# Two of the turns of a hybrid attention and convolution trunk, taken from TensorE to VectorE and a crossing through memory

## The chip, the cores and the metric

One core of a Trainium2 chip runs the whole program. The metric is device time in microseconds (us) from the first to the last instruction's end, median of several runs; lower is better. The engines are called as in the profile: PE is TensorE (PEld its weight loads), DVE is VectorE, ACT is ScalarE, POOL is GpSimd, and SP issues most of the transfers.

## The reference

A trunk of two layers on 256 tokens of 2048 features, float32. Cut to what matters here:

```
for layer in range(2):
    h = rms_norm(x, norm_g)                                  # 256 x 2048
    q, k, v, g_att, glu_a, glu_b, g_conv = split(h @ w_in)   # seven times 2048 columns
    att    = dilated_mixture(rope(rms(q)), rope(rms(k)), v)  # 16 heads of 128
    att_y  = rms_norm(att, att_out_g) * silu(g_att)          # the gated attention
    u      = glu_a * sigmoid(glu_b)                          # the gated unit
    y      = depthwise_conv(u, 31 taps, causal) + dw_bias
    y      = silu(layer_norm(y, ln_g, ln_b))
    conv_y = rms_norm(y @ w_pw, conv_out_g) * silu(g_conv)
    x      = x + concat(att_y, conv_y) @ w_out
```

## The kernel before

**Products.** Every projection is done in float32 precision by three products of float32r parts: the weights are split into `whi` (ACT, L238) and the rest `wlo` (DVE, L239), the activations into `st_hi` and `st_lo`, 128 features by 256 tokens each, and `whi*sthi + wlo*sthi + whi*stlo` is accumulated. A *tile* is 256 rows by 512 columns of a weight; it takes 12 matmuls of 512 columns (L669). A *group* is 8 tiles: 512 columns of one projection for all tokens. A layer has 40 groups: glu_b, glu_a, v, q, k for each of four column blocks j; then g_conv 0, g_att 0 to 3, g_conv 1 to 3; then o_att 0 to 3, pw 0 to 3, o_conv 0 to 3. There are 640 tiles in all. Weights are loaded by SP into four buffers `raw` (512 KB each); `split(i)` stands three tiles ahead of the products of tile i, and the load that reuses its buffer stands right behind it.

**Turns.** A projection leaves PE with tokens on the partitions. The convolution and the next product need features on the partitions. So the gated unit (`Dt[0]`, written by `ev_glu_a`), q, k, the gated attention (`A[j]`, written by `ev_g_att`), the result of pw and the new x are turned by PE: `transposes` (L280) makes 8 transposes of 128 x 128 for a block of 256 x 512, from where ACT (and DVE for `st_lo`) evict them. The function `to_stationary` does the turn and both parts; it waits until the stationary chunk is vacant, which for the gated attention is during g_conv 3.

**Convolution and norm.** `conv` runs 31 taps for each of four feature tiles of a block on DVE, the first tap as `V.tensor_scalar` (L403), the others as `scalar_tensor_tensor` (L406). Then POOL adds up the means (`ysum`), `ln_square` squares on ACT, `add_squares` sums the squares over features on POOL (L355, L357, into `ssum`), `token_sums` finishes on PE (L366), POOL makes the reciprocal root (`rsqrt`, and `rbc` at L441), PE spreads it (L445), and `ln_silu` makes the stationary parts that pw reads.

**Order.** The instruction streams are written in the order in which the Python code emits them. Between the tiles' products a planner, `Filler`, places everything else: each piece states its cost on an engine in a `Need` (P, V, A, G in us), and is emitted when the planner's clock for its inputs is past and the engine is not more than a horizon ahead (V 4.5 us, A 3.5 us). Each engine runs its stream in order.

Of the kernel before, what the change touches and what calls it, by code (L numbers as in the profile page):

```python
# [30 lines left out]

KS = 2
NSTEP = KT // KS
R_RAW, R_SPLIT = 4, 4
AHEAD = 3

WARM = 10
# [13 lines left out]
class Filler:  # L51
# [7 lines left out]

    def __init__(self, banks, horizon, patience):  # L60
        self.tasks = []
        self.t = dict(P=0.0, V=0.0, A=0.0, G=0.0)
        self.horizon, self.patience = horizon, patience
        self.banks = [(b, 0.0) for b in banks]
        self.count = 0
# [42 lines left out]
    def _fits(self, task):  # L108
        prio, _, _, need, ready = task
        now = self.t["P"]  # L110
        if not need.holds():
            return False
        if need.banks and sum(at <= now for _, at in self.banks) < need.banks:
            return False
        late = 0 if prio < self.patience else 2
        for n, (e, cost) in enumerate(need.time):
            if n == 0 and ready > (now if e == "P" else max(now, self.t[e]) + 0.2):
                return False
            e = "V" if e == "G" else e
            if e in self.horizon and max(self.t[e], ready) + cost > now + self.horizon[e] - late:  # L120
                return False
        return True
# [23 lines left out]
def trunk(ctx: ExitStack, tc: tile.TileContext, x, w_in, q_norm_g, k_norm_g, w_pw, w_out, x_t, gains, params,  # L146
# [8 lines left out]
    def t(shape, name, dt=F32):  # L155
        return sb.tile(shape, dt, name=name)
# [13 lines left out]
    qT, kT = (C[i].rearrange("p (h s) -> p h s", h=4) for i in (1, 2))  # L170
    Dt = [t([128, 2, CH], f"d{i}") for i in range(3)]
    t2 = t([128, CH], "t2")
    sm = [t([128, 384], f"sm{i}") for i in range(4)]
    junk = t([128, CH], "junk", BF16)
    ident = t([128, 128], "ident")
# [19 lines left out]

    acc = [pp.tile([128, CH], F32, name=f"acc{i}") for i in range(4)]
    fill = Filler([pp.tile([128, CH], F32, name=f"ax{i}") for i in range(4)], dict(V=4.5, A=3.5), 5)

    xs = [dr.tile([SEQ, CH], F32, name=f"xs{c}") for c in range(NCH)]

# [65 lines left out]
    def has(*what):  # L266
        return lambda: what in flags
# [6 lines left out]
    def transposes(src, banks):  # L274

        for b in range(2):
            for i in range(2):
                for tt in range(2):
                    e = (2 * b + i) * 128
                    T.transpose(banks[b][:, i * SEQ + tt * 128:i * SEQ + tt * 128 + 128],  # L280
                                src[:, tt, e:e + 128], ident)

    def to_stationary(src, s, c, gain):

        yield Need(2, lambda: vacant[s][c], P=0.9)
        banks = [fill.bank(), fill.bank()]
        transposes(src, banks)
        yield Need(A=1.5, V=1.6)
        p = [b[:, i * SEQ:(i + 1) * SEQ] for b in banks for i in range(2)]
        for i in range(4):  # L290
            S.activation(st_hi[s][c][:, i], p[i], AF.Copy, scale=gain(i))  # L291
        for i in range(4):
            V.scalar_tensor_tensor(st_lo[s][c][:, i], p[i], gain(i), st_hi[s][c][:, i].bitcast(F32),  # L293
                                   op0=ALU.mult, op1=ALU.subtract)
        fill.free(*banks)
        filled(s, c)

    def filled(s, c):
        vacant[s][c] = False
        ready[s][c] = True  # L300
# [17 lines left out]

    def x_chunk(l, c):

        yield from to_stationary(A[c], 0, c, lambda i: ng[:, l * KT + 4 * c + i:l * KT + 4 * c + i + 1])
        fill.add(x_square(l, c), 3, fill.now[4])

    def x_square(l, c):
# [24 lines left out]

    def add_squares(sq, j, *name):  # L350
        for h in range(2):
            yield Need(0, has(*name, j - 1) if j else None, G=1.3)
            half_sq = sq[:, h * CH:(h + 1) * CH]
            if j == 0 and h == 0:
                G.tensor_copy(ssum, half_sq)  # L355
            else:
                G.tensor_add(ssum, ssum, half_sq)  # L357
        flag(*name, j)

    def token_sums():  # L360
# [17 lines left out]
    def ev_glu_a(l, j, ps):  # L378
        yield Need(0, has("ev", l, "glu_b", j), V=1.4)
        for tt in range(2):  # L380
            V.scalar_tensor_tensor(Dt[0][:, tt], ps[tt], rx[:, tt:tt + 1], Dt[0][:, tt],
                                   op0=ALU.mult, op1=ALU.mult)
        flag("ev", l, "glu_a", j)
        yield Need(2, has("conv", l, j - 2) if j >= 2 else None, P=0.9)
        banks = [fill.bank(), fill.bank()]
        transposes(Dt[0], banks)
        yield Need(A=1.0)
        for b in range(2):
            S.activation(uT[j % 2][:, 2 * b:2 * b + 2, PAD:], banks[b].rearrange("p (c s) -> p c s", c=2), AF.Copy)
        fill.free(*banks)  # L390
        flag("glu", l, j)
        fill.add(conv(l, j), 5 + j, fill.now[4])

    def conv(l, j):
        u = uT[j % 2]
        y = Y[j].rearrange("p (c s) -> p c s", c=4)
        w = prm[:, 4 * j:4 * j + 4]
        for k in range(CW):
            for c in range(4):
                if c % 2 == 0:  # L400
                    yield Need(V=0.8)
                if k == 0:
                    V.tensor_scalar(y[:, c], u[:, c, 0:SEQ], w[:, c, l * CW:l * CW + 1], w[:, c, P_BIAS + l:P_BIAS + l + 1],  # L403
                                    op0=ALU.mult, op1=ALU.add)
                else:
                    V.scalar_tensor_tensor(y[:, c], u[:, c, k:k + SEQ], w[:, c, l * CW + k:l * CW + k + 1], y[:, c],  # L406
                                           op0=ALU.mult, op1=ALU.add)
        flag("conv", l, j)
        for c in range(4):
            yield Need(0, has("ysum", l, j - 1) if j else None, G=0.7)  # L410
            if j == 0 and c == 0:
                G.tensor_copy(ysum, y[:, c])
            else:
                G.tensor_add(ysum, ysum, y[:, c])  # L414
        flag("ysum", l, j)
        if j == NCH - 1:
            fill.add(layer_norm(l), 4, fill.now[4])
# [151 lines left out]
    def ev_g_att(l, j, ps):  # L569
        yield Need(0, has("attsq", l, j), A=1.2, V=1.2)  # L570
        for tt in range(2):
            S.activation(Dt[0][:, tt], ps[tt], AF.Silu, scale=rx[:, tt:tt + 1])
        V.tensor_mul(A[j], A[j], Dt[0])
        flag("ev", l, "g_att", j)
        yield from to_stationary(A[j], 0, j, lambda i: prm[:, 4 * j + i, P_ATT + l:P_ATT + l + 1])
        src = x[0, :, j * CH:(j + 1) * CH] if l == 0 else xs[j]
        nc.sync.dma_start(A[j], src.rearrange("(t p) e -> p t e", p=128))

# [6 lines left out]
    def ev_pw(l, j, ps):  # L585
# [6 lines left out]
        if j == NCH - 1:  # L592
# [1 line left out]
            V.tensor_reduce(rsc, ssf, axis=mybir.AxisListType.X, op=ALU.add)  # L594
            rsqrt(rc, rsc, 1.0 / D, 2)
            flag("rc", l)
        yield from to_stationary(y, 1, j, lambda i: prm[:, 4 * j + i, P_CONV + l:P_CONV + l + 1])

    def ev_o_conv(l, j, ps):
        yield Need(0, has("rc", l), V=1.4)  # L600
# [19 lines left out]
    load(2)  # L620
    load(3)
    x_load(2)
    make_identity(nc, ident)
    V.memset(half, -0.5)
    for u in uT:
# [10 lines left out]
                G.tensor_mul(rope[nm + part], rope[nm + part], gbc[:, None, :].to_broadcast([128, 2, DH]))  # L636

    split_first()


    users = {"glu_b": ev_glu_b, "glu_a": ev_glu_a, "v": ev_v, "g_conv": ev_g_conv, "g_att": ev_g_att,
# [3 lines left out]
    for i, (g, s) in enumerate(tiles):  # L645
# [4 lines left out]
            fill.until(has("ev", *groups[g - 2][:3]))  # L650
        for a in range(i + AHEAD if i else 1, i + AHEAD + 1):
            split(a)
            if a == 1:
                x_load(3)
            if a in (1, 4, 6):
                first_chunk((1, 4, 6).index(a) + 1)
        ps = [acc[(2 * g + tt) % 4] for tt in range(2)]
# [80 lines left out]
```

## Time and profile before

| | |
|---|---|
| median of 3 runs | 1853.83 us (1853.01 to 1854.2) |
| the profiled execution | 1854.28 us, of which the span from first to last instruction is 1852.5 us |
| PE busy | 1844.7 us, 8494 matmuls |
| DVE busy | 1397.7 us (75%) |
| ACT busy | 987.4 us (53%) |
| POOL busy | 142.3 us (8%) |
| granted TensorE clock | 1.000 of full speed |
| HBM | 188 GB/s over the span |

Busy time of PE is not work at its peak, since matmuls overlap: the recorded time of one is longer than the step from one to the next. So the chain of what ended last is read beside it. One profiled execution stands for the runs: its time is 0.45 us above their median.

### The profile page before, as it was taken

To read this page: it belongs to the slowest core of one execution; us is meant where nothing else is said; L and a number is where in the kernel's file an instruction comes from. 1 tells how busy PE (TensorE), PEld (TensorE's weight loads), DVE (VectorE), ACT (ScalarE), POOL (GpSimd) and SP (SyncE) were. 2 spreads that over 40 slices of the span, in tenths; PEclk is the share of its full clock that TensorE was granted. 3 is DMA by queue.
4 is the path that set the end of the run, shared out by engine and by line. 5 is a ranking of instruction groups with operands and counts; after the bars stand their busy time and mean duration, and the time that the engine had idled before them with its cause. 6 is when DMAs were issued, how large, how long until landed. Compare 5 with 4: busy or idle time off the path is not lost.

```text
span 1852.5 us, 23729 instructions
## 1 busy us (share of the span) xinstructions
PE 1844.7 (100%) x8494; PEld 1534.4 (83%) x8494; DVE 1397.7 (75%) x2162; ACT 987.4 (53%) x1549; POOL 142.3 (8%) x153
## 2 busy tenths in 40 slices
PE   9999999999999999999999999999999999999999
PEld 6888888888888888888888888888888888888887
DVE  6888889788889876555558888797887998755554
ACT  6465564655644465445444655646556445644542
POOL 0210100200010140000000101002001002100000
PEclk9999999999999999999999999999999999999999
DMA  8655656556566676555666556565565666665564
GB/s 276 211 183 162 189 157 197 183 161 192 162 191 194 193 221 210 194 183 196 208 202 193 183 162 191 159 194 181 161 192 160 194 195 190 213 204 195 176 205 146
DMA packets 180599, 349.97 MB, mean 189 GB/s; under 512 B 11216, under 2 KB 11216, under 8 KB 180480
## 3 DMA queue, kind: packets, MB, share of 16 engines
q1 hardware_dynamic: 178512, 345.09, 59.6%
q0 software_dynamic: 960, 1.77, 0.5%
q8 instruction: 66, 1.08, 0.2%
q10 hardware_dynamic: 1008, 1.59, 0.2%
q14 instruction: 53, 0.43, 0.1%
HBM read 344.21 MB, written 4.19 MB: 188 GB/s over the span
## 4 chain that ended last, share of the span: by engine, by line
PE 99%; DMA 0%; DVE 0%; ACT 0%; ACTq 0%; issue 0%
PE acc L669 94%; PE ax L280 2%; PE ax L517 1%; PE ax L534 1%; PE ax L543 0%; PE ax L542 0%; PE ax L541 0%; PE ax L516 0%; DMA y<-in_x_t 0%; PE ax L366 0%; DVE wlo L239 0%; PE ax L445 0%; PE ax L422 0%; DVE stlo L307 0%; DVE a L602 0%; ACT whi L249 0%
## 5 line engine op out<-in xcount | busy, mean ns | idle before, releaser
L239 DVE TENSOR_TENSOR wlo<-raw,whi 128x1024 fp32r<-128x1024 f32 x639 | 792.0, 1248 | 392.2 <-ACT whi L238 386.0
L238 ACT ACTIVATE whi<-raw 128x1024 fp32r<-128x1024 f32 x639 | 674.6, 1063 | 658.1 <-PE acc L669 480.6
L669 PE MATMUL acc<-whi,sthi 128*128 128x512 f32 x2560 | 822.6, 392 | 2.0 <-ACT whi L249 2.0
L669 PE MATMUL acc<-wlo,sthi 128*128 128x512 f32 x2560 | 814.9, 389 | 0.3 <-DVE wlo L239 0.3
L669 PE MATMUL acc<-whi,stlo 128*128 128x512 f32 x2560 | 814.7, 389 | 0.0
L669 PEld LDWEIGHTS acc<-wlo,sthi 128*128 128x128 f32 x2560 | 480.4, 188 | 101.7 <-DVE wlo L250 0.9
L669 PEld LDWEIGHTS acc<-whi,stlo 128*128 128x128 f32 x2560 | 480.6, 188 | 100.4
L669 PEld LDWEIGHTS acc<-whi,sthi 128*128 128x128 f32 x2560 | 475.8, 188 | 98.0 <-ACT whi L249 3.3
L406 DVE SCALAR_TENSOR_TENSOR y<-ut,prm,y 128x256 f32<-128x256 f32 x960 | 410.1, 485 | 0.0
L414 POOL TENSOR_TENSOR ysum<-ysum,y 128x256 f32<-128x256 f32 x30 | 36.6, 1218 | 240.9 <-DVE y L406 131.6
L479 POOL TENSOR_SCALAR qr<-qss 128x8 f32<-128x8 f32 x16 | 3.1, 197 | 663.7 <-ACT junk L476 663.7
L476 ACT ACTIVATE junk<-acc,rx 128x128 bf16<-128x128 f32 x128 | 47.0, 367 | 8.4 <-PE acc L669 4.8
L486 ACT ACTIVATE d<-acc,qr 128x128 f32<-128x128 f32 x128 | 34.7, 383 | 16.9 <-POOL qr L481 16.9
L291 ACT ACTIVATE sthi<-ax,prm 128x256 fp32r<-128x256 f32 x64 | 25.1, 475 | 30.7 <-PE ax L280 30.7
L293 DVE SCALAR_TENSOR_TENSOR stlo<-ax,prm,sthi 128x256 fp32r<-128x256 f32 x64 | 26.5, 475 | 14.4 <-ACT sthi L291 14.4
L507 ACT ACTIVATE c<-ax 128x512 f32<-128x512 f32 x32 | 17.4, 596 | 33.7 <-PE ax L280 33.7
L530 ACT ACTIVATE sm<-sm,smm 128x128 f32<-128x128 f32 x64 | 28.2, 442 | 6.6 <-DVE smm L525 6.6
L357 POOL TENSOR_TENSOR ssum<-ssum,d 128x512 f32<-128x512 f32 x14 | 28.5, 2036 | 6.5 <-ACT d L435 5.6
L480 POOL TENSOR_TENSOR qr<-qr,half 128x8 f32<-128x8 f32 x16 | 26.3, 1643 | 1.3
L280 PEld LDWEIGHTS ax<-ident,d 128*128 128x128 f32 x192 | 22.4, 140 | 3.2
L280 PE MATMUL ax<-ident,d 128*128 128x128 f32 x192 | 24.9, 273 | 0.0
L476 ACT ACTIVATION_READ_ACCUMULATOR junk<-acc,rx 128x1 f32 x128 | 24.7, 193 | 0.0
(112 smaller groups left out, 666.7 us busy)
## 6 DMA issues: line engine op xcount, KB each, us to landing
raw<-in_w_in SPq DMA_DIRECT2D x447, 512.0 KB, 3.8
raw<-in_w_out SPq DMA_DIRECT2D x128, 512.0 KB, 4.7
raw<-in_w_pw SPq DMA_DIRECT2D x64, 512.0 KB, 4.7
a<-in_x SPq DMA_DIRECT2D x4, 512.0 KB, 5.7
xs<-a SPq DMA_DIRECT2D x4, 512.0 KB, 6.7
a<-xs SPq DMA_DIRECT2D x4, 512.0 KB, 5.6
y<-in_x_t SPq DMA_DIRECT2D x3, 512.0 KB, 7.2
out<-a SPq DMA_DIRECT2D x4, 256.0 KB, 4.9
```

What stands on the lines that cost most here:

```text
L238: S.activation(hi, a, AF.Copy)
L239: V.tensor_sub(wlo[i % R_SPLIT], a, hi.bitcast(F32))
L280: T.transpose(banks[b][:, i * SEQ + tt * 128:i * SEQ + tt * 128 + 128], src[:, tt, e:e + 128], ident)
L293: V.scalar_tensor_tensor(st_lo[s][c][:, i], p[i], gain(i), st_hi[s][c][:, i].bitcast(F32), op0=ALU.mult, op1=ALU.subtract)
L357: G.tensor_add(ssum, ssum, half_sq)
L406: V.scalar_tensor_tensor(y[:, c], u[:, c, k:k + SEQ], w[:, c, l * CW + k:l * CW + k + 1], y[:, c], op0=ALU.mult, op1=ALU.add)
L414: G.tensor_add(ysum, ysum, y[:, c])
L476: S.activation(junk[:, :DH], ps[tt][:, h * DH:(h + 1) * DH], AF.Square, scale=rx[:, tt:tt + 1], accum_out=qss[:, tt, h:h + 1])
L480: G.tensor_tensor(qr, qr, half.rearrange("p (t h) -> p t h", t=2), op=ALU.pow)
L486: S.activation(n[:, tt, h * DH:(h + 1) * DH], ps[tt][:, h * DH:(h + 1) * DH], AF.Copy, scale=qr[:, tt, h:h + 1])
L530: S.activation(s[:, cs], s[:, cs], AF.Exp, bias=m[:, tt:tt + 1], scale=-1.0, accum_out=lsum[:, tt:tt + 1])
L669: T.matmul(ps[tt], xl if n == 2 else xh, lo[:, kk] if n == 1 else hi[:, kk], start=(k == 0 and n == 0), stop=(k == KT - 1 and n == 2))
```

## The change

The gated unit and the gated attention are no longer turned on PE. DVE transposes each 32 x 32 square of the block on its own (`V.transpose`, two instructions of 128 x 512, into a new tile `blocks`), a transfer on SP's queue writes `blocks` to a buffer in memory, `crossing`, and four transfers read it back with the squares in their new places. The planner has a new clock Q for such transfers: the write is emitted when the transposes' planned end is past, the reads 9.0 us after the write, and what uses the result 13.0 us after the reads. The turned block lies as `(a c t j)`, so ACT and DVE read it through a view (`turned`).

With it: the first tap of the convolution goes from DVE to ACT; the sums of squares of the layer norm go from POOL to DVE, with the first copy folded into the first addition; `raw` has five buffers instead of four (room comes from a smaller descriptor scratch of POOL's transfers), so load(4) stands ahead of the first split, and x_load(3) behind it.

```diff
-R_RAW, R_SPLIT = 4, 4
+R_RAW, R_SPLIT = 5, 4
...
-            if n == 0 and ready > (now if e == "P" else max(now, self.t[e]) + 0.2):
+            if n == 0 and ready > (now if e in "PQ" else max(now, self.t[e]) + 0.2):
...
+    crossing = [dr.tile([4, 128, SEQ], F32, name=f"crossing{i}") for i in range(2)]
+    turns = [0, False]
...
+    def turn(src, dst):
+        yield Need(0, lambda: not turns[1], V=1.4)
+        turns[1] = True
+        for tt in range(2):
+            V.transpose(blocks.rearrange("p (b c t j) -> p t c b j", b=4, c=4, t=2)[:, tt],
+                        src[:, tt].rearrange("p (c b j) -> p c b j", c=4, b=4))
+        yield Need(Q=9.0)
+        way = crossing[turns[0] % 2]
+        turns[0] += 1
+        nc.sync.dma_start(way.rearrange("b p x -> p b x"), blocks.rearrange("p (b x) -> p b x", b=4))
+        yield Need(Q=13.0)
+        turns[1] = False
+        for a in range(4):
+            nc.sync.dma_start(dst[:, a * SEQ:(a + 1) * SEQ], way[:, 32 * a:32 * a + 32])
+
+    def turned(z):
+        return z.rearrange("p (a c t j) -> p c t a j", a=4, c=4, t=2)
+
+    def to_stationary_turned(src, dst, s, c, gain):
+        yield from turn(src, dst)
+        yield Need(0, lambda: vacant[s][c], A=1.8, V=2.2)
+        z = turned(dst)
+        hi, lo = (o[s][c].rearrange("p c (t a j) -> p c t a j", t=2, a=4) for o in (st_hi, st_lo))
+        for i in range(4):
+            S.activation(hi[:, i], z[:, i], AF.Copy, scale=gain(i))
+        for i in range(4):
+            for tt in range(2):
+                V.scalar_tensor_tensor(lo[:, i, tt], z[:, i, tt], gain(i), hi[:, i, tt].bitcast(F32),
+                                       op0=ALU.mult, op1=ALU.subtract)
+        filled(s, c)
...
     def add_squares(sq, j, *name):
         for h in range(2):
-            yield Need(0, has(*name, j - 1) if j else None, G=1.3)
             half_sq = sq[:, h * CH:(h + 1) * CH]
             if j == 0 and h == 0:
-                G.tensor_copy(ssum, half_sq)
-            else:
-                G.tensor_add(ssum, ssum, half_sq)
+                continue
+            yield Need(0, has(*name, j - 1) if j else None, V=0.7)
+            V.tensor_add(ssum, half_sq, sq[:, :CH] if j == 0 else ssum)
...
-        yield Need(2, has("conv", l, j - 2) if j >= 2 else None, P=0.9)
-        banks = [fill.bank(), fill.bank()]
-        transposes(Dt[0], banks)
-        yield Need(A=1.0)
-        for b in range(2):
-            S.activation(uT[j % 2][:, 2 * b:2 * b + 2, PAD:], banks[b].rearrange("p (c s) -> p c s", c=2), AF.Copy)
-        fill.free(*banks)
+        z = Dt[0].rearrange("p t e -> p (t e)")
+        yield from turn(Dt[0], z)
+        yield Need(0, has("conv", l, j - 2) if j >= 2 else None, A=1.7)
+        for c in range(4):
+            S.activation(uT[j % 2][:, c, PAD:].rearrange("p (t a j) -> p t a j", t=2, a=4), turned(z)[:, c], AF.Copy)
...
                 if k == 0:
-                    V.tensor_scalar(y[:, c], u[:, c, 0:SEQ], w[:, c, l * CW:l * CW + 1], w[:, c, P_BIAS + l:P_BIAS + l + 1],
-                                    op0=ALU.mult, op1=ALU.add)
+                    if c == 0:
+                        yield Need(A=1.9)
+                    S.activation(y[:, c], u[:, c, 0:SEQ], AF.Identity, scale=w[:, c, l * CW:l * CW + 1],
+                                 bias=w[:, c, P_BIAS + l:P_BIAS + l + 1])
...
-        yield from to_stationary(A[j], 0, j, lambda i: prm[:, 4 * j + i, P_ATT + l:P_ATT + l + 1])
+        yield from to_stationary_turned(A[j], A[j].rearrange("p t e -> p (t e)"), 0, j,
+                                        lambda i: prm[:, 4 * j + i, P_ATT + l:P_ATT + l + 1])
+        yield Need(Q=1.0)
...
-    nc = bacc.Bacc("TRN2", target_bir_lowering=False, num_devices=1)
+    nc = bacc.Bacc("TRN2", target_bir_lowering=False, num_devices=1, dynamic_dma_scratch_size=4096)
```

Three places in the order of instructions. The first is PE during g_conv 3 of layer 0, where the gated attention's first chunk is turned: `a0` is the gated attention, `ax` the banks for turns, `acc` the accumulators. Before:

```order
L669 MATMUL acc3_156<-whi1_94,stlo00_73 128x512
L280 MATMUL ax2_159<-ident_116,a0_85 128x128 x4
L280 MATMUL ax3_160<-ident_116,a0_85 128x128 x4
L669 MATMUL acc2_155<-whi2_95,sthi01_66 128x512
L669 MATMUL acc3_156<-whi2_95,sthi01_66 128x512
```

The same place with the change:

```order
L712 MATMUL acc3_158<-whi1_95,stlo00_73 128x512
L712 MATMUL acc2_157<-whi2_96,sthi01_66 128x512
L712 MATMUL acc3_158<-whi2_96,sthi01_66 128x512
L712 MATMUL acc2_157<-wlo2_100,sthi01_66 128x512
L712 MATMUL acc3_158<-wlo2_100,sthi01_66 128x512
```

The eight transposes are gone, and the products of the next tile follow at once. Of the 352 transposes of L280, 224 are left.

The second place is SP's queue in the group behind the first glu_a of layer 0, where there were only loads of weights. Before:

```order
L224 DMA raw3_92<-in_w_in 128x2x512
L224 DMA raw0_89<-in_w_in 128x2x512
L224 DMA raw1_90<-in_w_in 128x2x512
L224 DMA raw2_91<-in_w_in 128x2x512
L224 DMA raw3_92<-in_w_in 128x2x512
```

With the change:

```order
L228 DMA raw0_89<-in_w_in 128x2x512
L299 DMA crossing0_163<-blocks_112 128x4x256
L228 DMA raw1_90<-in_w_in 128x2x512
L228 DMA raw2_91<-in_w_in 128x2x512
L228 DMA raw3_92<-in_w_in 128x2x512
L303 DMA d0_108<-crossing0_163 128x1x256 x4
L228 DMA raw4_93<-in_w_in 128x2x512
```

The write stands between two loads, and its four reads three loads later; each load stands for one tile.

The third place is DVE in the layer norm of layer 0, from the token sums (`rsc`) to the first stationary part that pw reads (`stlo10`); each `wlo` row is one tile's split. Before:

```order
L369 COPY rsc_137<-ax2_159 128x2
L239 TENSOR_TENSOR wlo3_100<-raw3_92,whi3_96 128x1024
L239 TENSOR_TENSOR wlo0_97<-raw0_89,whi0_93 128x1024
L239 TENSOR_TENSOR wlo1_98<-raw1_90,whi1_94 128x1024
L239 TENSOR_TENSOR wlo2_99<-raw2_91,whi2_95 128x1024
L582 SCALAR_TENSOR_TENSOR a0_85<-acc0_153,ra_134,a0_85 128x512
L582 SCALAR_TENSOR_TENSOR a0_85<-acc1_154,ra_134,a0_85 128x512
L455 TENSOR_TENSOR y0_81<-y0_81,nmean_126 128x1024
```

With the change, the last sums and the same stretch:

```order
L397 TENSOR_TENSOR ssum_130<-d2_110,ssum_130 128x512
L243 TENSOR_TENSOR wlo2_100<-raw1_90,whi2_96 128x1024
L243 TENSOR_TENSOR wlo3_101<-raw2_91,whi3_97 128x1024
L409 COPY rsc_139<-ax2_161 128x2
L243 TENSOR_TENSOR wlo0_98<-raw3_92,whi0_94 128x1024
L243 TENSOR_TENSOR wlo1_99<-raw4_93,whi1_95 128x1024
L243 TENSOR_TENSOR wlo2_100<-raw0_89,whi2_96 128x1024
L624 SCALAR_TENSOR_TENSOR a2_87<-acc0_155,ra_136,a2_87 128x512
L624 SCALAR_TENSOR_TENSOR a2_87<-acc1_156,ra_136,a2_87 128x512
L495 TENSOR_TENSOR y0_81<-y0_81,nmean_128 128x1024
```

Here the chain has moved 16 tiles later, from the eviction of o_att 0 to that of o_att 2. On PE the token sums stood after 227 tiles and the spread root after 231; now they stand after 245 and 247. The first `stlo10` stood behind the split of tile 236 and now stands behind that of 252; pw reads it from tile 256.

## Rows read from the trace of the kernel before

**Rows 1.** The page: busy time of the engines, and granted clock in 40 slices.

```profile
PE 1844.7 (100%) x8494; PEld 1534.4 (83%) x8494; DVE 1397.7 (75%) x2162; ACT 987.4 (53%) x1549; POOL 142.3 (8%) x153
...
PEclk9999999999999999999999999999999999999999
```

**Rows 2.** The page: the chain that ended last, by engine.

```profile
PE 99%; DMA 0%; DVE 0%; ACT 0%; ACTq 0%; issue 0%
```

**Rows 3.** The same chain in order of time: start us, length us, what.

```profile
648.05 0.87 PE ax L280 x8
648.93 5.46 PE acc L669 x24
654.38 0.87 PE ax L280 x8
...
682.00 138.74 PE acc L669 x612
```

**Rows 4.** Instructions by line and shape, PE's transposes: busy us, mean ns.

```profile
L280 PE MATMUL ax<-ident,d 128*128 128x128 f32 x192 | 24.9, 273 | 0.0
...
L280 PE MATMUL ax<-ident,a 128*128 128x128 f32 x96 | 12.4, 272 | 0.0
```

**Rows 5.** Who waited for whom: us in total, times, longest us.

```profile
ACT whi L238 <- PE acc L669: 480.6, 328, 2.6
DVE wlo L239 <- ACT whi L238: 386.0, 290, 3.9
...
PEld acc L669 <- DVE wlo L239: 0.7, 1, 0.7
```

**Rows 6.** Instructions by line and shape, DVE, ACT and POOL.

```profile
L239 DVE TENSOR_TENSOR wlo<-raw,whi 128x1024 fp32r<-128x1024 f32 x639 | 792.0, 1248 | 392.2 <-ACT whi L238 386.0 <-PE acc L669 4.1
L238 ACT ACTIVATE whi<-raw 128x1024 fp32r<-128x1024 f32 x639 | 674.6, 1063 | 658.1 <-PE acc L669 480.6 <-DVE y L406 164.1 <-DVE a L602 9.2
...
L357 POOL TENSOR_TENSOR ssum<-ssum,d 128x512 f32<-128x512 f32 x14 | 28.5, 2036 | 6.5 <-ACT d L435 5.6
L293 DVE SCALAR_TENSOR_TENSOR stlo<-ax,prm,sthi 128x256 fp32r<-128x256 f32 x64 | 26.5, 475 | 14.4 <-ACT sthi L291 14.4
...
L403 DVE TENSOR_SCALAR y<-ut,prm 128x256 f32<-128x256 f32 x32 | 14.3, 494 | 0.0
...
L525 DVE CUSTOM_DVE_ANT_0 sm<-ax,mask 128x128 f32<-128x128 f32 x32 | 9.3, 292 | 4.4 <-PE ax L517 4.1
L389 ACT ACTIVATE ut<-ax 128x512 f32<-128x512 f32 x16 | 8.7, 596 | 16.8 <-PE ax L280 16.8
...
L314 ACT ACTIVATE sthi<-y,ng 128x256 fp32r<-128x256 f32 x12 | 5.1, 495 | 0.0
...
L345 DVE TENSOR_TENSOR ssum<-d 128x512 f32<-128x512 f32 x1 | 0.7, 691 | 0.0
```

**Rows 7.** Busy time by stage, g_att to g_conv 2 of layer 0.

```profile
508.00:636.00 128.00, 128.00 (x567) 106.03 (x565) 113.11 (x183) 57.44 (x62) 9.88 (x9) 1.00 0.65 193
```

**Rows 8.** Transfers: SP's queue (packets, MB, share), issues (KB, us to landing).

```profile
q1 hardware_dynamic: 178512, 345.09, 59.6%
...
xs<-a SPq DMA_DIRECT2D x4, 512.0 KB, 6.7
a<-xs SPq DMA_DIRECT2D x4, 512.0 KB, 5.6
```

**Rows 9.** The tile `raw`: landing of its loads.

```profile
DMA to landing us min/median/max: 3.4/4.2/8.1
```

**Rows 10.** Timeline of PE, DVE and POOL in layer 0's norm: start us, length us.

```profile
669.61 0.95 PE L366 MATMUL ax<-ones,ssum 128*128 128x2 f32 x8
...
672.04 0.15 DVE L369 COPY rsc<-ax 128x2 f32<-128x2 f32 x1
...
673.33 0.40 POOL L441 COPY rbc<-rstd 128x256 f32<-128x256 f32 x1
...
681.39 0.61 PE L445 MATMUL ax<-ident,rbc 128*128 128x128 f32 x4
```

More of the change, by code (lines that the diff above doesn't have):

```diff
@@ L61, in __init__ @@
         self.tasks = []
-        self.t = dict(P=0.0, V=0.0, A=0.0, G=0.0)
+        self.t = dict(P=0.0, V=0.0, A=0.0, G=0.0, Q=0.0)
         self.horizon, self.patience = horizon, patience
@@ L172, in trunk @@
     t2 = t([128, CH], "t2")
+    blocks = t([128, 2 * CH], "blocks")
     sm = [t([128, 384], f"sm{i}") for i in range(4)]
@@ L319, in x_chunk @@
     def x_chunk(l, c):
-        yield from to_stationary(A[c], 0, c, lambda i: ng[:, l * KT + 4 * c + i:l * KT + 4 * c + i + 1])
+        gain = lambda i: ng[:, l * KT + 4 * c + i:l * KT + 4 * c + i + 1]
+        yield from to_stationary(A[c], 0, c, gain)
         fill.add(x_square(l, c), 3, fill.now[4])
@@ L399, in conv @@
             for c in range(4):
-                if c % 2 == 0:
-                    yield Need(V=0.8)
                 if k == 0:
-                    V.tensor_scalar(y[:, c], u[:, c, 0:SEQ], w[:, c, l * CW:l * CW + 1], w[:, c, P_BIAS + l:P_BIAS + l + 1],
-                                    op0=ALU.mult, op1=ALU.add)
-                else:
+                    if c == 0:
+                        yield Need(A=1.9)
+                    S.activation(y[:, c], u[:, c, 0:SEQ], AF.Identity, scale=w[:, c, l * CW:l * CW + 1],
+                                 bias=w[:, c, P_BIAS + l:P_BIAS + l + 1])
+                else:
+                    if c % 2 == 0:
+                        yield Need(V=0.8)
                     V.scalar_tensor_tensor(y[:, c], u[:, c, k:k + SEQ], w[:, c, l * CW + k:l * CW + k + 1], y[:, c],
@@ L596, in ev_pw @@
             flag("rc", l)
-        yield from to_stationary(y, 1, j, lambda i: prm[:, 4 * j + i, P_CONV + l:P_CONV + l + 1])
+        gain = lambda i: prm[:, 4 * j + i, P_CONV + l:P_CONV + l + 1]
+        yield from to_stationary(y, 1, j, gain)
     def ev_o_conv(l, j, ps):
@@ L622, in trunk @@
     x_load(2)
+    load(4)
     make_identity(nc, ident)
@@ L638, in trunk @@
     split_first()
+    x_load(3)
     users = {"glu_b": ev_glu_b, "glu_a": ev_glu_a, "v": ev_v, "g_conv": ev_g_conv, "g_att": ev_g_att,
@@ L652, in trunk @@
             split(a)
-            if a == 1:
-                x_load(3)
             if a in (1, 4, 6):
```

## The prediction

> **What bounds the kernel now.** The page first: PE is busy for 1844.7 of 1852.5 us and its granted clock is full, the higher of its two levels, in every slice [rows 1]. Since recorded matmuls overlap, busy time alone proves nothing; the chain that ended last does: 99% of the span is PE waiting for nobody [rows 2]. So time is won by taking work off PE's stream, and lost only where PE is made to wait. What does an instruction cost there? In the chain in order of time the reader is to see a regular step [rows 3]: in a stretch without anything else 612 products take 138.74 us, 0.2267 us each, so a tile of 12 takes 2.72 us. Where a turn stands in between, its 8 transposes are 0.87 us of the chain, and from one turn's start to the next (24 products between) it is 654.38 - 648.05 = 6.33 us, of which 24 products are 5.44: a turn costs PE **0.89 us**, the 0.02 over 0.87 lying in the products behind it.
>
> Then the waits [rows 5]. PE waited for DVE's split once, 0.7 us. ACT on the other hand waited for PE in 328 of 639 splits: it starts when PE gives a buffer free. Such a split is due three tiles later, 8.16 us; ACT's half takes 1.06 and DVE's 1.25 [rows 6], so about 5.8 us are spare on DVE and 7.1 on ACT. That is the reserve which every delay below must use up before PE stops. DVE is the engine with least of it: 113.11 of 128 us busy in the densest stage [rows 7].
>
> **What comes off PE.** 16 turns: four blocks, two uses, two layers, 128 of 352 transposes. 16 x 0.89 = **14.2 us**. Nothing is put on PE in their place, and its other instructions stay in their order but for the norm's, below. One rule would make more of it. The records give each transpose 272 to 273 ns [rows 4]; 128 of them by that are 34.9 us. But records overlap: 8 of them fill 2.18 us and take 0.87 of the chain. I take the chain; the other is a rival.
>
> **What goes on DVE.** 32 square transposes: no row shows one. Nearest is a pass over 128x512 float32, 0.691 us [rows 6]; half of that, or twice it if filling and emptying the squares don't overlap, are the bounds: 22.1 us, from 11 to 44. The sums of squares: 14 passes of 128x512 at 0.691, 9.7 us, in place of POOL's 28.5. The gated attention's low parts: 64 instructions of 128x128 at 0.292 are 18.7, in place of 32 at 0.475, 15.2: 3.5 more. The first taps go: 14.3 less. In all 21 us more (10 to 43), 1397.7 to about 1419, 77% of a span of 1838. That is a mean; the place matters. A turn puts 1.4 us (0.7 to 2.8) behind glu_a's or g_att's eviction, inside 5.8 us of reserve even at the upper bound, and the planner defers taps when DVE's stream is full. So it costs nothing; without the cover a turn would cost up to 1.4 us. What becomes late is the end of the convolution and with it the norm. In the order the norm's first part for pw is 16 tiles later, and stands behind the split of tile 252 where pw needs it at 256. Splits run three to four tiles ahead, so it is done near tile 250: some 5 tiles, 13 us, remain. It still hides, but of the slack of some 20 tiles most is gone.
>
> **What goes on ACT.** First taps: 32 of 128x256 from SBUF at 0.495 [rows 6], 15.8 us. Copies of the gated unit: another 32, 15.8, for 16 from PSUM, 8.7. The gated attention's high parts keep their count. About 23 us on 987, against 7.1 us of reserve; at most 2 us stand in one piece. Nothing.
>
> **What goes on the queue.** SP gets 16 writes and 64 reads; each round trip is 512 KB out and 512 KB in. Price of a packet: 59.6% of 16 engines over 1852.5 us by 178,512 packets [rows 8] is 99 ns for 2 KB. The crossing moves rows of 1 KB, 512 packets each way; a packet lies between 50 (by bytes) and 99 ns (by count). On 16 engines that is 32 packets, 1.6 to 3.2 us. A load of 16 packets is 1.6 us and lands in 4.2 [rows 9], so 2.6 is fixed and a leg lands in 4.2 to 5.8; the same bytes in 2 KB rows took 6.7 out and 5.6 in [rows 8]. I take 6 to 7. The planner leaves 9.0 and 13.0, so neither SP nor ACT should stand at these transfers. The queue's share rises by 16 x 2 x (1.6 to 3.2) us, 3 to 6 points. Loads issued behind the reads are later by the reads' time; with five buffers a load is issued 5 x 2.72 - 2.31 = 11.3 us before its split can begin (8.6 with four) and lands in 4.2, at worst 8.1, so 3 to 7 us are free, and then the split's own reserve. Nothing at the start: PE's first products wait for the first two transfers and splits, whose place doesn't change. POOL loses 29 us that nobody waited for.
>
> **Sum.** 1854.28 of the profiled execution - 14.2 = **1840.1 us**. That execution is 0.45 us above the median of the runs, from which the same subtraction gives 1839.6. A measurement of this kernel tells about 0.2%, 3.7 us, from no change.
>
> **Rivals.**
> (a) *The norm makes PE wait.* PE takes its instructions in order, so the token sums and the spread root stop it if POOL and DVE are late. Before, from the token sums' end (670.56) to `rbc`'s (673.73) went 3.2 us, and PE spread it at 681.39, 7.7 us later [rows 10]. Now two tiles, 5.4 us, lie between instead of four, with DVE freshly behind seven sums. For it: the gap is halved. Against: 2.2 us are still left, and a sum takes 0.69 where POOL's took 2.04. If DVE is its full horizon of 4.5 us late, PE loses 2.3 us at the sums and as much at the root, in two layers: 9 us, 1849; at half of that 1844.5.
> (b) *The reads are slow, and the kernel slower.* The read's source begins with a dimension of 4, its target with 128 partitions. If only 4 of the 16 engines carry a read, and the four reads the same four, each has 128 packets: 6.3 us at 50 ns, 12.7 at 99. At 50 a read lands in 8.9, within 13. At 99 it lands in 15.3, and ACT, in order, stands 2.3 us at the copies, within 7.1; and the next load, behind the reads in the queue, comes 12.7 + 1.6 - 2.7 = 11.6 us late, lands in 15.8, makes its split 4.5 us late, of 5.8 in reserve. So PE begins to lose at 109 ns a packet, 0.128 us a turn for each ns more; over 116 ns the 0.89 is spent. At 125 ns: 16 x 2.05 = 33 us lost, 1873. Against it: a packet of half the bytes would have to take longer than the mean of the whole ones. The Trainium skill, "DMA: Bandwidth & Descriptors", section "Why a DMA increments its semaphore by 16 and not by 1", says that a transfer is spread over the largest number of engines up to 16 that divides the slowest dimension of both sides, which here is 4; no row of this trace shows a transfer of that shape, and by this rule alone the reads land in 8.9 to 15.3 us, not in 6, and the sum stays.
> (c) *A transpose costs its record.* 34.9 us go: 1819. Against it, the steps of rows 3. The Trainium skill, "TensorE: Matmul & The Clock Gate", section "Part 4: PE-mode transpose", gives some 275 ns for one of 128x128 in a kernel; the trace's records agree (272 to 273), its chain doesn't (109 each in a turn), and an estimate by the page, 128 x 0.275, is 35.2 us.
> (d) *No change.* If something else paced PE, the 14.2 us would turn into waits: 1854. Rows 2 and 5 show nothing that could.
>
> **How the numbers follow.** Forecast 0.79; (a) 0.10; (b) 0.05; (c) 0.03; (d) 0.03. Forecast by itself: 1838.5 (0.93 a turn, and the median's 0.45 less) to 1842.5 (DVE late by 2 us at one place). The range reaches into (a), to 1844.5, and leaves out its worst, (b), (c) and (d): 1838.5 to 1844.5. Faster by over 0.2%: forecast, (a), (c) and some of the rest, 0.92; within: (d) and a mild (b), 0.04; slower: the rest of (b), 0.04.
>
> **What would show it.** Right: the chain still 99% PE, with 28 pieces of turns instead of 44 and the products' step still 0.2267; PE's matmuls 128 fewer; PE not waiting for DVE, ACT or a transfer. For the terms: the square transpose at 0.5 to 0.9 us; the write landing within 9 us, the reads within 13; DVE near 1419. Wrong by (a): waits of PE at the token sums or the spread root. By (b): ACT waiting for `crossing`, SP for its write, landings of `raw` above 11. By anything else: a step of the products other than 0.2267.

## The result, and the profile after

| | before | after |
|---|---|---|
| median | 1853.47 us (4 runs, 1853.01 to 1854.20) | 1839.99 us (4 runs, 1839.64 to 1840.06) |
| ratio | | 0.9925 [0.9914, 0.9937] |
| the profiled execution, its span | 1854.28, 1852.5 us | 1840.05, 1838.3 us |

The kernel is faster by 0.75%, 13.5 us; forecast were 1840.1 us. The page of the kernel after answers to [rows 1, 2 and 8]: busy time, the chain by engine, SP's queue.

```profile
PE 1830.8 (100%) x8366; PEld 1521.0 (83%) x8366; DVE 1404.6 (76%) x2208; ACT 1006.4 (55%) x1597; POOL 110.5 (6%) x137
...
PE 99%; DMA 0%; DVE 0%; ACT 0%; ACTq 0%; issue 0%
...
q1 hardware_dynamic: 195408, 361.87, 63.9%
```

PE has 128 matmuls fewer and still makes 99% of the chain, in which 28 pieces of turns are left of 44. The same chain in order of time, through the layer norm of layer 0 and to the next turn that PE still makes, in place of [rows 3]:

```profile
503.58 185.00 PE acc L712 x816
688.57 0.43 PE ax L462 x2
689.00 21.80 PE acc L712 x96
710.80 0.99 PE ax L406 x8
711.79 5.56 PE acc L712 x24
717.35 0.45 PE ax L485 x4
717.80 95.22 PE acc L712 x420
813.02 0.87 PE ax L284 x8
813.89 5.49 PE acc L712 x24
```

The first piece shows it best: 185.00 us by 816 products are 0.2267 each, as before, and it goes through all of layer 0's gated attention without one turn. The turns that are left take 0.87 as before. The token sums (L406) take 0.99 in place of 0.79, and the waits say why: in both layers together PE's weight loads waited 0.7 us for the last sum of DVE. That row, and those that answer to [rows 5], from the table of waits:

```profile
ACT whi L242 <- PE acc L712: 482.6, 335, 2.8
DVE wlo L243 <- ACT whi L242: 368.1, 285, 3.9
...
PEld ax L406 <- DVE ssum L397: 0.7, 2, 0.4
PEld acc L712 <- DVE wlo L243: 0.7, 1, 0.7
```

I compared the starts of each tile's first product in the two traces. Each of the 16 places of a turn that was taken away is 0.80 us shorter, and the tile behind it 0.10: 16 x 0.90 = 14.4 us. The token sums give back 0.2 in each layer. The other pieces of the norm stand at later tiles with the lengths that they had, and all other tiles stand as they stood. That makes 14.0; from the second tile's first product to the last tile's the stretch is 13.9 us shorter, and the span 14.2, since the second tile began 0.7 us earlier (10.8 for 11.6; over the kernels here it begins between 10.3 and 11.9) and the span ended 0.4 later behind the last product (4.5 for 4.1).

The new instructions, from the groups by line and shape (busy us, mean ns of one, idle before), beside the splits, in place of [rows 6]:

```profile
L243 DVE TENSOR_TENSOR wlo<-raw,whi 128x1024 fp32r<-128x1024 f32 x639 | 779.5, 1228 | 372.8 <-ACT whi L242 368.1 <-PE acc L712 2.2
...
L319 DVE SCALAR_TENSOR_TENSOR stlo<-a,prm,sthi 128x128 fp32r<-128x128 f32 x64 | 17.5, 344 | 0.0
...
L441 ACT ACTIVATE y<-ut,prm 128x256 f32<-128x256 f32 x32 | 16.5, 587 | 0.0
...
L428 ACT ACTIVATE ut<-d 128x256 f32<-128x256 f32 x32 | 10.6, 403 | 0.3 <-DMA d<-crossing 0.3
...
L294 DVE STREAM_TRANSPOSE blocks<-a 128x512 f32<-128x512 f32 x16 | 10.4, 691 | 0.3
L294 DVE STREAM_TRANSPOSE blocks<-d 128x512 f32<-128x512 f32 x16 | 10.3, 684 | 0.0
...
L397 DVE TENSOR_TENSOR ssum<-d,ssum 128x512 f32<-128x512 f32 x12 | 8.3, 688 | 0.3
```

A square transpose of 128x512 takes what a pass over 128x512 takes. Only 0.3 us in the whole run did ACT wait for a crossing.

### The profile page after: what moved, and what is told of

Its sections match the earlier page's. It is cut to its first block, busy times and chain, and to the rows that moved or that the text cites. A ratio compares the mean times of both kernels' runs of the same rounds, so it can differ in the third digit from the quotient of the medians.

```text
span 1838.3 us, 23657 instructions
## 1 busy us (share of the span) xinstructions
PE 1830.8 (100%) x8366; PEld 1521.0 (83%) x8366; DVE 1404.6 (76%) x2208; ACT 1006.4 (55%) x1597; POOL 110.5 (6%) x137
## 4 chain that ended last, share of the span: by engine, by line
PE 99%; DMA 0%; DVE 0%; ACT 0%; ACTq 0%; issue 0%
PE acc L712 95%; PE ax L284 1%; PE ax L557 1%; PE ax L574 1%; PE ax L583 0%; PE ax L582 0%; PE ax L581 0%; PE ax L556 0%; DMA y<-in_x_t 0%; PE ax L406 0%; DVE wlo L243 0%; PE ax L485 0%; PE ax L462 0%; DVE stlo L347 0%; DVE a L645 0%; ACT whi L253 0%
## 5 line engine op out<-in xcount | busy, mean ns | idle before, releaser
L243 DVE TENSOR_TENSOR wlo<-raw,whi 128x1024 fp32r<-128x1024 f32 x639 | 779.5, 1228 | 372.8 <-ACT whi L242 368.1
L454 POOL TENSOR_TENSOR ysum<-ysum,y 128x256 f32<-128x256 f32 x30 | 29.8, 994 | 393.0 <-DVE y L446 278.8
L333 DVE SCALAR_TENSOR_TENSOR stlo<-ax,prm,sthi 128x256 fp32r<-128x256 f32 x32 | 13.3, 478 | 13.7 <-ACT sthi L331 13.7
L565 DVE CUSTOM_DVE_ANT_0 sm<-ax,mask 128x128 f32<-128x128 f32 x64 | 20.3, 355 | 3.8 <-PE ax L557 3.2
L539 DVE TENSOR_TENSOR d<-d,t 128x512 f32<-128x512 f32 x32 | 22.1, 692 | 1.1
L595 ACT ACTIVATE junk<-a 128x512 bf16<-128x512 f32 x16 | 10.1, 632 | 22.7 <-DVE a L586 22.4
L331 ACT ACTIVATE sthi<-ax,prm 128x256 fp32r<-128x256 f32 x32 | 12.5, 474 | 16.8 <-PE ax L284 16.8
```

Of the source, the lines that this page charges most:

```text
L243: V.tensor_sub(wlo[i % R_SPLIT], a, hi.bitcast(F32))
L539: V.tensor_add(ot, ot, t2v)
L565: V.tensor_tensor_reduce(s[:, cs], ps[:, cs], mask[:, cs], -1.0, 3e38, op0=ALU.add, op1=ALU.min, accum_out=m[:, tt:tt + 1])
```

## The experiments

My theory was: the time is PE's stream alone; the turns' 0.89 us each are the whole gain, everything else of the change is hidden and only has to stay hidden. Against it stood that the other parts (sums, tap, buffer) bring something themselves, and rival (b), that the reads use few engines of the transfers and stand near a threshold. Times are medians; each ratio is to runs of the kernel before that were taken along with them.

**All but the turns.** The gated unit and the gated attention are turned by PE again; sums, tap and five buffers stay.

```diff
-        yield from turn(Dt[0], z)
...
+        transposes(Dt[0], banks)
...
-        yield from to_stationary_turned(A[j], A[j].rearrange("p t e -> p (t e)"), 0, j,
...
+        yield from to_stationary(A[j], 0, j, lambda i: prm[:, 4 * j + i, P_ATT + l:P_ATT + l + 1])
```

> All edits of the change but the turns, which are PE's transposes again (first tap on ACT, sums of squares on DVE, five weight buffers stay). Theory (PE's 128 transposes are the whole gain, 0.89 us a turn): 1854, within 0.2% of the kernel before, with 44 pieces of turns in PE's chain. Rival (the other edits carry a part, through a lighter POOL and earlier loads): below 1850.

Measured: 1854.98 us beside 1853.85, ratio 1.0007 [0.9998, 1.0017]. These parts alone bring nothing that can be told. All 44 pieces of turns are back, and from the second tile's first product to the last tile's PE takes 1834.0 us in both traces; what this trace has more lies behind the last product, 5.5 us for 4.1.

**The turns alone.** Sums on POOL, tap on DVE, four buffers, as before; the turns as after.

```diff
-R_RAW, R_SPLIT = 5, 4
+R_RAW, R_SPLIT = 4, 4
...
+                G.tensor_add(ssum, ssum, half_sq)
...
+                    V.tensor_scalar(y[:, c], u[:, c, 0:SEQ], w[:, c, l * CW:l * CW + 1], w[:, c, P_BIAS + l:P_BIAS + l + 1],
```

> The turns alone go to DVE and the crossing; first tap on DVE, sums on POOL and four weight buffers as before. Theory: 1840 (1839 to 1842), the same as the whole change, since DVE's 22 us more lie in its reserve. Rival (the turns need the relief of the other edits, because DVE keeps 14 us of taps and loads behind the reads come late with four buffers): over 1843, with PE waiting for DVE or ACT.

Measured: 1841.25 us (1841.03 to 1841.40), ratio 0.9933 [0.9919, 0.9948], 1.3 us over the kernel after. Its waits:

```profile
ACT whi L242 <- DMA raw<-in_w_in: 36.8, 16, 3.8
...
PEld acc L711 <- DVE stlo L501: 2.7, 3, 1.4
...
PE acc L711 <- DVE stlo L501: 1.4, 2, 1.0
```

With four buffers ACT waits for loads, 3.8 us at the longest and within its reserve; PE loses nothing by it. But pw's first products now wait for the norm's low part. The timeline of DVE and PE where pw begins in layer 0 (start us, length us):

```profile
742.55 1.21 DVE L501 TENSOR_TENSOR stlo<-y,sthi 128x1024 fp32r<-128x1024 f32 x1
...
743.82 0.72 PE L711 MATMUL acc<-whi,stlo 128*128 128x512 f32 x2 [0.96 <-DVE stlo L501]
```

In the kernel after the same instruction begins at 726.12, 16 us earlier. So the turns alone bring 12.6 us where the whole change brings 13.5, and the other parts together pay for the lateness that the turns make: PE's tiles 256, 576 and 578 were longer by 1.26, 0.71 and 0.33 us.

**One other part undone at a time.** Four buffers; the sums of squares on POOL; the first tap on DVE.

```diff
-R_RAW, R_SPLIT = 5, 4
+R_RAW, R_SPLIT = 4, 4
```

> The changed kernel with four weight buffers. In the changed kernel a turn's reads move 512 packets in some 7 us, about four at a time. A load issued 2.7 us behind them would land about 6 us late, in 10.3 us, against 8.6 us from issue to split with four buffers: splits 1.7 us late, inside the usual 5.8 us of reserve. Theory: 1840 to 1841, ACT waiting for raw a few times. Rival (the reserve is thinner where the reads fall): 1843 or more.

```diff
-            V.tensor_add(ssum, half_sq, sq[:, :CH] if j == 0 else ssum)
+            if j == 0 and h == 0:
+                G.tensor_copy(ssum, half_sq)
+            else:
+                G.tensor_add(ssum, ssum, half_sq)
```

> The changed kernel with the sums of squares on POOL again; the first tap stays on ACT. POOL's sums take 2.04 us each where DVE's take 0.69. Theory (the norm has some 5 tiles of slack at pw, 13 us): the norm comes 2 to 3 tiles later and is still in time, 1840.0 to 1840.5. Rival (this edit alone kept it in time): PE waits for stlo at pw's first tile, 1841 or more.

```diff
-                    S.activation(y[:, c], u[:, c, 0:SEQ], AF.Identity, scale=w[:, c, l * CW:l * CW + 1],
-                                 bias=w[:, c, P_BIAS + l:P_BIAS + l + 1])
+                    V.tensor_scalar(y[:, c], u[:, c, 0:SEQ], w[:, c, l * CW:l * CW + 1], w[:, c, P_BIAS + l:P_BIAS + l + 1],
+                                    op0=ALU.mult, op1=ALU.add)
```

> The changed kernel with the first tap on DVE again; the sums of squares stay on DVE. 7.2 us a layer more on DVE ahead of the norm. Theory (the same slack): 3 tiles later and still in time, 1840.0 to 1840.5; only both together used the slack up, with 2.3 us of waits at pw in the kernel with the turns alone. Rival: PE waits for stlo at pw's first tile, 1841 or more.

| undone | median | ratio to before | first low part of pw begins |
|---|---|---|---|
| fifth buffer | 1840.31 us | 0.9929 [0.9914, 0.9944] | |
| sums on DVE | 1838.87 us | 0.9918 [0.9902, 0.9935] | 731.12 |
| tap on ACT | 1840.03 us | 0.9926 [0.9912, 0.9941] | 734.99 |
| none (the kernel after) | 1839.99 us | 0.9925 [0.9914, 0.9937] | 726.12 |

None alone changes the time by what can be told from its ratio. The sums on POOL came out below what was expected (1840.0 to 1840.5): in that trace PE has no wait at the token sums, which in the kernel after cost 0.2 us a layer, and the end behind the last product is 0.4 us shorter; so beside the other two parts the move of the sums may even have cost something. Four buffers make ACT wait for landings, as the waits of that kernel show, and PE not:

```profile
ACT whi L242 <- DMA raw<-in_w_in: 51.6, 23, 4.2
...
ACT whi L242 <- DMA raw<-in_w_out: 8.3, 5, 2.8
```

The sum on POOL costs the norm 5 us and the tap on DVE 9 us of nearly 16 that it has until pw, and each alone stays inside. All three parts undone together ran over; pairs of them were not tried.

**One of the two turns.** The gated unit by PE, the gated attention by the crossing.

```diff
-        yield from turn(Dt[0], z)
...
+        transposes(Dt[0], banks)
```

> The changed kernel with the gated unit turned by PE again; only the gated attention crosses. Theory (each turn is worth 0.89 us wherever it stands): 8 turns are left out of the gain, 1840.0 + 7.1 = 1847.1. Rival (the gated attention's turns, in the stage where DVE is fullest, are worth less or more than the unit's): below 1845 or above 1849.

Measured: 1847.16 us (1846.72 to 1847.67), ratio 0.9965 [0.9952, 0.9978]. Eight turns bring half of what sixteen bring: the price is one per turn, whichever of the two it is.

**The reads on more engines.** One read whose slowest dimension is 128 in place of four with 4; for this the write puts the squares elsewhere, in four transfers.

```diff
+        nc.sync.dma_start(dst.rearrange("p (a x) -> p a x", a=4), way.rearrange("a q x -> q a x"))
...
-            nc.sync.dma_start(dst[:, a * SEQ:(a + 1) * SEQ], way[:, 32 * a:32 * a + 32])
```

> The changed kernel with the crossing laid out so that four writes of 32 partitions and one read of 128 partitions take the place of one write and four reads; the read's slowest dimension is now 128 on both sides. In the changed kernel the four reads' 512 packets took 7 us, four at a time. Theory (only a few engines carried them, and it was hidden anyway): the read's packets run some 16 at a time and are through in 2 to 4 us, and the time stays at 1840.0 (1839.5 to 1840.5). Rival (the long reads did hold back loads): 1839 or less.

Measured: 1840.20 us (1839.51 to 1842.72), ratio 0.9930 [0.9914, 0.9947], the same. The records of the reads' packets of 1 KB, in the gated unit's turn that is written at 176 us:

```
                 from the (first) read's issue    a packet   at a time   most at once
after, reads     +2.55 to  +9.81 us               56 ns      3.9         7
one read         +2.31 to  +5.06 us               46 ns      8.5         20
                 512 packets each; "at a time" is the mean from the first packet to the last
```

Over all 16 turns the four reads were done 9.1 to 11.3 us after the first one's issue, 3.4 to 4.3 packets at a time and at most 8 at once, 50 to 62 ns each; the one read 4.1 to 6.7 us after it, 5.2 to 11.5 at a time and 18 to 21 at the most crowded moment of a turn, 46 to 51 ns. From its first packet to its last the one read took 2.1 to 4.5 us, about what was expected. So what rival (b) supposed is there: the four reads run about four packets at a time, as four engines would carry them (the records don't name the engine), and they land where it said, in 8.9 to 15.3. The rule of the Trainium skill that the prediction named ("DMA: Bandwidth & Descriptors", section "Why a DMA increments its semaphore by 16 and not by 1") says 4 engines for these reads and 16 for the one. The trace agrees with the first, and shows more than four at work in the second, though not how many. What did not come is its price: the packet took 50 to 62 ns, and (b) begins at 109.

**The reads doubled.** To see whether that threshold is real, four more reads of the same bytes stand ahead of the four, into a tile `dump` that nothing uses.

```diff
+    dump = t([128, 2 * CH], "dump")
...
+        for a in range(4):
+            nc.sync.dma_start(dump[:, a * SEQ:(a + 1) * SEQ], way[:, 32 * a:32 * a + 32])
         for a in range(4):
             nc.sync.dma_start(dst[:, a * SEQ:(a + 1) * SEQ], way[:, 32 * a:32 * a + 32])
```

> The changed kernel with four more reads of the same rows into an unused tile ahead of the four real ones, 1024 packets a turn on the same few engines. By the price of the changed kernel (57 ns a packet, four at a time) they take 14.6 us: the real ones land near 18 us, ACT stands some 5 us at the gated unit's copies, and a load behind comes 13 us late, its split 6 to 7 us late of 5.8 in reserve. Theory (reads become dear where they use up that reserve): 0.5 to 1 us lost a turn, 1848 to 1856. Rival (loads pass the reads, so that only ACT's own wait counts, inside its 7.1 us): 1840 to 1842.

Measured: 1871.74 us (1869.52 to 1873.11), ratio 1.0097 [1.0082, 1.0112]: 31.8 us slower than after. The direction was as expected, the size was not. The waits of this kernel, ACT's, PE's and SP's own:

```profile
ACT whi L243 <- DMA raw<-in_w_in: 88.3, 32, 11.7
...
ACT ut L431 <- DMA d<-crossing: 44.2, 8, 6.0
...
PEld acc L715 <- ACT whi L243: 18.0, 8, 3.5
PE acc L715 <- ACT whi L243: 14.6, 8, 3.1
...
SPq L229 <- DMA raw<-in_w_in: 64.8, 16, 5.6
```

The gated unit's eight turns show one half of (b): ACT stood some 5.5 us each at the copies, for the crossing. Behind six of them PE lost 0.2 us at the most. Behind the last one of each layer the copies and four first taps stand in front of the next split; in layer 0 it began at 442.14, 7.2 us behind its step and so just over the 7.1 us of reserve, and PE lost 1.3 us there in each layer. The gated attention's eight show the other half: ACT stood up to 11.7 us at a split whose load came late, more than its reserve, and there lie 28 of the 31 us that PE lost. What I had left out is that SP issues in order and waits. The timeline of SP in one such turn:

```profile
566.58 2.27 SPq L304 DMA_DIRECT2D dump<-crossing  x4
568.90 5.04 SPq L306 DMA_DIRECT2D a<-crossing  x4
574.04 3.98 SPq L229 DMA_DIRECT2D raw<-in_w_in  x4
```

Eight reads keep SP for 7.4 us, where four kept it for 2.3, and the load behind them is issued at 574.04; its split begins at 584.95, when ACT has stood for it for 11.3 us. The load was late by its place in the queue and by its issue. SP's own waits for loads (the last row above) held back what stood behind them as well. Then the second part of the loss, which the windows of PE show (columns: the window and its length; busy time and instructions of PE, PEld, DVE, ACT and POOL; granted clock; share and GB/s of the transfers):

```profile
571.00:579.00 8.00, 8.00 (x37) 6.60 (x37) 6.39 (x10) 1.07 (x1) 0.00 (x0) 1.00 0.52 149
579.00:587.00 8.00, 5.38 (x22) 3.80 (x20) 0.97 (x1) 1.73 (x2) 0.00 (x0) 0.95 1.06 308
587.00:595.00 8.00, 7.90 (x30) 6.32 (x30) 8.00 (x16) 5.48 (x7) 0.00 (x0) 0.84 0.65 210
595.00:603.00 8.00, 8.00 (x37) 6.60 (x37) 7.97 (x13) 3.48 (x4) 0.00 (x0) 1.00 0.49 158
```

Behind the stop the granted clock is 0.84 in a window of which PE is busy for 7.90 of 8.00 us, and 30 products pass in place of 37. How the 31 us divide into standing and clock was not worked out.

**More turns through the crossing.** With the one read, also the first three blocks of pw's result and of the new x: 9 turns more.

```diff
-        yield from to_stationary(y, 1, j, gain)
+        if j < 3:
+            yield from to_stationary_turned(y, Y[j], 1, j, gain)
+        else:
+            yield from to_stationary(y, 1, j, gain)
```

> With the crossing of one read, the result of pw and the new x also cross, for the first three of four blocks, whose 20 us of latency lie before the next stage reads them: 6 + 3 more turns. Theory (each is worth 0.89 us on PE as long as nothing is late; DVE is half idle in this stage): 1840.0 - 8.0 = 1832.0. Rival (the third block's turn is late for the stage that follows): PE waits for stlo there, 1834 or more.

Measured: 1832.31 us (1831.37 to 1832.67), ratio 0.9884 [0.9870, 0.9899]. PE's stream is 7.99 us shorter than after, at just these nine places: 0.89 each.

**And q and k.** On top of it the 16 turns of q and k; q and k share `blocks` and the crossing with the gated unit. `raw` keeps its five buffers.

```diff
-        yield Need(2, has("qk", l, j - 1) if j else None, P=0.9)
-        banks = [fill.bank(), fill.bank()]
-        transposes(o, banks)
...
+        yield from turn(o, qz if nm == "q" else C[2], ("rope", l, j, nm))
```

> As the kernel with pw and x crossing, and q and k cross too: 16 more turns; q lands in a tile of its own and ACT copies it, k is read by PE through the turned view. Theory: 1832.0 - 14.2 = 1818 if the attention's heads, some 25 us later, stay ahead of their evictions and DVE (11 us of square transposes a layer more) keeps its splits in time. Rival (with k's evictions waiting behind q's turn, or a fuller DVE and a later norm, PE waits): 1822 to 1840.

Measured: 1864.54 us (1864.11 to 1865.93), ratio 1.0060 [1.0045, 1.0075]. Both expectations were wrong. The turns did go from PE, at 0.90 each; but what rival (a) of the prediction named came, and much larger than it said. The waits:

```profile
PEld acc L723 <- ACT sthi L508: 21.5, 4, 7.0
PE acc L723 <- ACT sthi L508: 20.1, 4, 6.8
...
PE ax L413 <- DVE ssum L404: 11.4, 2, 8.5
...
PE ax L492 <- POOL rbc L488: 4.8, 2, 3.0
```

PE stands at the token sums, at the spread root and at pw's first tiles: these tiles are 27.5 us longer in layer 0 and 21.7 in layer 1, of which 1.6 each is the norm's own work on PE, which stood at earlier tiles. The windows around layer 0's norm show that not all of it is standing:

```profile
730.00:733.00 3.00, 3.00 (x15) 2.49 (x14) 1.72 (x3) 1.54 (x2) 1.43 (x1) 1.00 0.56 174
733.00:736.00 3.00, 0.69 (x4) 0.23 (x2) 1.63 (x2) 1.97 (x3) 2.18 (x4) 1.00 0.62 187
736.00:739.00 3.00, 0.00 (x0) 0.00 (x0) 2.90 (x4) 0.98 (x2) 0.72 (x1) 0.73 0.38 93
739.00:742.00 3.00, 0.00 (x0) 0.00 (x0) 3.00 (x5) 0.00 (x0) 0.00 (x0) 0.50 0.58 184
742.00:745.00 3.00, 1.86 (x8) 1.78 (x8) 0.27 (x2) 0.00 (x0) 0.59 (x2) 0.50 0.37 132
...
754.00:757.00 3.00, 3.00 (x8) 2.32 (x9) 2.13 (x2) 0.68 (x1) 0.00 (x0) 0.50 0.00 0
757.00:760.00 3.00, 3.00 (x13) 2.41 (x12) 0.16 (x1) 1.26 (x2) 0.00 (x0) 0.85 0.52 175
```

PE stood from 733.7, and its granted clock fell to 0.50, the lower of its two levels; it was still there when the products began again. The chain shows the price at the token sums, which took 0.99 in the kernel after, and at the 12 products of pw's first tile, which take 2.72 elsewhere:

```profile
742.16 1.88 PE ax L413 x8
...
753.79 4.93 PE acc L723 x12
```

**Only q.** The nine and the 8 turns of q; k stays on PE.

```diff
+        if nm == "q":
+            yield Need(0, has("qk", l, j - 1) if j else None, V=0.0)
+            yield from turn(o, qz, ("rope", l, j, nm))
...
+        else:
+            yield Need(2, has("qk", l, j - 1) if j else None, P=0.9)
+            banks = [fill.bank(), fill.bank()]
+            transposes(o, banks)
```

> The kernel with pw and x crossing, and of q and k only q crosses (8 turns more, 5.5 us of square transposes a layer on DVE; k stays with PE so that its evictions wait for nobody). Theory (each turn is worth 0.89 us as long as the norm is in time): 1832.3 - 7.1 = 1825.2. Rival (the norm of pw, which every DVE microsecond ahead of it pushes back, has no slack left: its first part would stand at pw's first product): PE waits there, 1827 to 1840.

Measured: 1824.79 us (1824.26 to 1825.27), ratio 0.9843 [0.9828, 0.9857], the fastest of all: 1.6% under the kernel before and 0.8% under the one after. PE's stream is 6.89 us shorter than with the nine. Beside the wait at the token sums, which the kernel after has too, PE's weight loads now wait a little for the spread root:

```profile
PEld ax L413 <- DVE ssum L404: 0.6, 1, 0.6
PEld ax L492 <- POOL rbc L488: 0.4, 1, 0.4
```

The two kernels differ in k's way alone, so k's turns make the norm late. How far shows on DVE: the last tap of layer 0's convolution ends at 678.9 us with the nine, at 688.9 with q and at 710.9 with q and k, and on PE the token sums stand after 245, 249 and 256 tiles, the last directly ahead of pw. Eight turns of k move the convolution's end by 22 us where q's moved it by 10. That is more than the 5.5 us a layer of their square transposes; where the rest comes from was not separated.

## Why the prediction was right

*What bounds the kernel.* Right. As long as PE isn't made to wait, its stream decides: 0, 8, 16, 25 and 33 turns taken away gave, against the kernel before, -1.1, 6.7, 13.5, 21.2 and 29.2 us, 0.84 to 0.88 a turn for the last four. The -1.1 is not in the stream, which is as long as before.

*0.89 us a turn.* Right: 0.90 by the tiles, 0.80 where the turn stood and 0.10 behind it. The 14.2 were 14.4, of which 0.4 went back at the token sums. That the median lies 0.1 us from the forecast is in part luck: the forecast started from an execution 0.8 us above the median of the four runs before, the token sums' wait was not in it, nor was the end, 0.4 us longer. From 1853.47 the stretch's 13.9 lead to 1839.6.

*DVE.* The engine's sum was too high, 1419 for 1404.6, and one step is most of the reason: I kept the splits as they were. They fell from 792.0 [rows 6] to 779.5 us. With the sums on POOL again (the experiment above) they take 791.5, so POOL's sums had been slowing them. The prediction took POOL's 29 us for work that nobody waited for; DVE paid 12 us for them. The transposes were taken at the right value of the range from 0.35 to 1.4: 20.7 us for 22.1. The low parts have records of 344 ns for 292, but follow one another closer: 17.5 us for 18.7. It cost nothing, as forecast.

*ACT.* 1006.4 for about 1010. First taps take 0.587 us for 0.495, the copies 0.403 for 0.495.

*The queue.* The share rose by 4.3 points, of 3 to 6. The write's packets were through in 4.7 to 7.8 us, inside 9. For the reads "6 to 7" was wrong: 9.1 to 11.3, inside the planner's 13 and so without a price. The step that failed is the spreading over 16 engines; the bounds of rival (b) held them.

*The reserve.* It hides what it was said to hide, ACT's 5.5 us at most copies of the doubled reads, and breaks where it was said to break: a split 7.2 us late cost PE 1.3 us. But the prediction set ACT's largest piece at 2 us against it, and the copies and first taps of one block stand together, 3.4 us. And in what a late load costs, SP's own time to issue the reads was missing, 0.5 us each.

*The norm.* 13 us of slack were forecast; the first low part was done at 727.35, and the first product that reads it stood at 743.04, so 15.7. Rival (a) came at its first place with 0.2 us a layer, not 2.3. Where q and k were added it came with some 46 us, far over the 9 of its worst: it had DVE late by the planner's horizon, not by a convolution that ends 32 us later.

Rivals (c) and (d) fell: records of 272 to 273 ns stand for steps of 0.11 us in the chain, and 14 and not 35 us went. The Trainium skill's 275 ns ("TensorE: Matmul & The Clock Gate", section "Part 4: PE-mode transpose") agree with the records; the estimate by them, 35.2 us, is not what went.

## What to carry to other kernels

Where the chain of what ended last is one engine alone, price an edit by the step in that chain, not by the records' lengths, and it adds up turn by turn, until the work that you moved makes some other thing late. So keep an account of the slack at each place where the full engine meets the others: here the norm's, nearly 16 us. Each help (sums, tap, buffer) was worth nothing alone, and all three undone cost 1.3 us; whether the later turns need them all was not tried. A transfer may take half as long again as you thought and cost nothing, or be doubled once more and cost 32 us: ask for its threshold, not for its time.

## What the runs showed of the hardware

POOL's sums beside DVE made DVE's splits longer. In the kernel with the sums on POOL again, DVE and POOL in layer 0's norm:

```profile
696.95 4.56 DVE L243 TENSOR_TENSOR wlo<-raw,whi 128x1024 fp32r<-128x1024 f32 x2
...
702.75 11.30 DVE L243 TENSOR_TENSOR wlo<-raw,whi 128x1024 fp32r<-128x1024 f32 x6
...
696.02 15.81 POOL L398 TENSOR_TENSOR ssum<-ssum,d 128x512 f32<-128x512 f32 x7
```

The first two splits, all beside POOL's sums, take 2.28 us each in place of 1.22; the next six, the last of them no longer beside the sums, 1.88 on the mean. POOL's sum takes 2.26 where DVE's takes 0.69. Over the whole trace 14 splits overlap a sum of POOL; 12 of them have records of 2.31 to 2.32 us, the other two of 1.21. Moving the sums put 9.6 us on DVE and took 12 from it.

A stop of PE costs more than the stop: where the norm was late the granted clock was 0.50 when the products began again, and the next tile took 2.2 us more.
